# Adaptive max pooling: one flat input in two groups, one reduction per load, three stores

## The chip, the cores and the metric

The kernel runs on one core of one Trainium2 chip. The metric is device time in microseconds, the median of several executions. The span, which the profile uses, goes from the first to the last instruction of the program and is about 1.8 us shorter. A run counts as fast when it is within 1.5% of the fastest run of the same kernel.

## The reference

The length of 4096 is cut into 256 windows of 16, and each window gives its maximum. As a flat array the input is 2,097,152 windows of 16 float32 (134.2 MB), the output one float32 for each (8.39 MB).

```python
batch, channels, length = 32, 256, 4096        # x: float32; output_size = 256
for i in range(output_size):
    start = int(i * length / output_size)
    end = int((i + 1) * length / output_size)
    result[:, :, i] = np.max(x[:, :, start:end], axis=-1)
```

## The kernel before

The 8192 rows are read in three groups of 21 rows per partition, and 128 rows remain. In a group, partition p starts 21 x 16 KB = 336 KB after partition p - 1: that distance is called the *partition pitch* here. A load takes three rows per partition (48 KB) into a ring that holds three such loads, and VectorE reduces each row by itself. The stores are issued after all loads.

```python
    RING = 9
    G = 21
    N_GROUPS = 3
    LOAD = 3
    CUT = 15
    ...
    ring = pool.tile([P, RING, O, W], fp32, tag="ring", name="ring")
    ...
    xg = xf[0:main].rearrange("(g p r) (o w) -> g p r o w", p=P, r=G, w=W)
    ...
    for g in range(N_GROUPS):
        for r in range(0, G, LOAD):
            at = n_read % RING
            nc.sync.dma_start(
                out=ring[:, at : at + LOAD], in_=xg[g][:, r : r + LOAD]
            )
            for i in range(LOAD):
                pooled(outs[g][:, (r + i) * O : (r + i + 1) * O], ring[:, at + i])
            n_read += LOAD
    ...   # the remaining 128 rows: one load of 16 KB per partition, one reduction
    ...   # five stores: groups 0 and 1, group 2 in two parts, the remaining rows
```

## Time and profile before

| | before |
|---|---|
| time | 335.93 us (335.87 to 336.12, 3 runs) |
| span | 334.3 us |
| DMA queue of loads and stores | 98.9% of 16 engines' span |
| VectorE busy | 278.8 us, 83% |
| bytes | 134.2 MB read, 8.39 MB written |

The page of the kernel before, parts 1, 2, 3 and 5. In part 2 each digit is the busy share, in tenths, of one of 40 slices of the span (9 is 90% or more), and the GB/s row is what the 16 DMA engines moved in that slice.

```profile
span 334.3 us, 157 instructions
DVE 278.8 (83%) x64; POOL 0.2 (0%) x4
...
DMA  9899999999999999999999999999999999999997
GB/s 371 382 465 453 400 465 394 453 459 394 465 394 453 459 394 465 394 453 459 394 465 394 453 459 394 465 394 448 459 400 459 400 447 459 400 459 388 437 426 297
...
q1 hardware_dynamic: 3744, 142.48, 98.9%
...
L53 DVE TENSOR_REDUCE out<-ring 128x256 f32<-128x4096 f32 x63 | 274.5, 4412 | 47.6 <-DMA ring<-in_x_dram 47.6
```

DMA is at 9 in 38 of the 40 slices, VectorE (DVE) was busy for 83% of the span, and all of VectorE's 47.6 us of idle time before reductions was ended by the landing of a load. GB/s alternates because a packet is 48 KB and is counted in the slice where it starts; the mean matters. The chain of waits says the same in order of time (start, duration, what):

```profile
1.64 45.82 DMA ring<-in_x_dram
...
47.48 13.08 DVE out L53 x3
...
60.58 30.47 DMA ring<-in_x_dram
...
91.08 13.08 DVE out L53 x3
```

A chain that alternates between DMA and VectorE looks as if both were limits. It isn't so: the links are 43.6 us apart and pass over three loads (30.47 + 13.08 us). The slot that a reduction frees is filled 30.5 us later because two other loads are queued ahead. One load per 14.53 us, 6.29 MB each, is 433 GB/s: that is the period, and three reductions need only 13.08 us of it.

### The profile page before, as it was taken

The numbers are of one execution on the slowest core, as the hardware profiler recorded it, in microseconds if no ns is written. First come the engines' busy times: TensorE is split into PE (matmuls) and PEld (weight loads), VectorE is DVE, ScalarE is ACT, GpSimd is POOL, SyncE is SP. The second block draws the span as 40 slices with busy tenths as digits, with TensorE's granted clock in tenths as the row PEclk, the third lists the DMA queues.
The fourth block names the chain that finished last, engine by engine and source line by source line (L and its number), as shares of the span: only waits on it lengthen the run. The fifth ranks groups of instructions, "written<-read, shape, count | busy, mean of one in ns | idle before, by whom it ended". The sixth has DMA issues, their size and how long they took to land.

```text
span 334.3 us, 157 instructions
## 1 busy us (share of the span) xinstructions
DVE 278.8 (83%) x64; POOL 0.2 (0%) x4
## 2 busy tenths in 40 slices
DVE  0078989898898989889898898989889898988990
POOL 0000000000000000000000000000000000000000
DMA  9899999999999999999999999999999999999997
GB/s 371 382 465 453 400 465 394 453 459 394 465 394 453 459 394 465 394 453 459 394 465 394 453 459 394 465 394 448 459 400 459 400 447 459 400 459 388 437 426 297
DMA packets 3889, 142.62 MB, mean 427 GB/s; under 512 B 432, under 2 KB 560, under 8 KB 688
## 3 DMA queue, kind: packets, MB, share of 16 engines
q1 hardware_dynamic: 3744, 142.48, 98.9%
q10 hardware_dynamic: 144, 0.13, 0.1%
q14 instruction: 1, 0.01, 0.0%
HBM read 134.22 MB, written 8.39 MB: 427 GB/s over the span
## 4 chain that ended last, share of the span: by engine, by line
DMA 68%; DVE 26%; DVEq 2%; SPq 0%; issue 0%
DMA ring<-in_x_dram 68%; DVE out L53 25%; DVEq L109 2%; DVE ring L53 1%; SPq L59 0%
## 5 line engine op out<-in xcount | busy, mean ns | idle before, releaser
L53 DVE TENSOR_REDUCE out<-ring 128x256 f32<-128x4096 f32 x63 | 274.5, 4412 | 47.6 <-DMA ring<-in_x_dram 47.6
L53 DVE TENSOR_REDUCE ring<-ring 128x256 f32<-128x4096 f32 x1 | 4.4, 4410 | 0.0
L95 POOL MEMSET const-bfloat16-1.0<- 128x1 bf16 x1 | 0.1, 101 | 0.0
L95 POOL MEMSET const-uint8-127<- 128x1 uint8 x1 | 0.1, 101 | 0.0
L95 POOL MEMSET const-float32-0.0<- 128x1 f32 x1 | 0.1, 98 | 0.2 <-issue 0.2
L95 POOL MEMSET const-float32-1.0<- 128x1 f32 x1 | 0.1, 98 | 0.0
## 6 DMA issues: line engine op xcount, KB each, us to landing
ring<-in_x_dram SPq DMA_DIRECT2D x21, 6144.0 KB, 30.5
out_dram<-out SPq DMA_DIRECT2D x2, 2688.0 KB, 38.4
ring<-in_x_dram SPq DMA_DIRECT2D x1, 2048.0 KB, 29.5
out_dram<-out SPq DMA_DIRECT2D x1, 1920.0 KB, 38.2
out_dram<-out SPq DMA_DIRECT2D x1, 768.0 KB, 11.2
out_dram<-ring ACTq DMA_DIRECT2D x1, 128.0 KB, 6.4
```

What stands on the lines that cost most here:

```text
L53: nc.vector.reduce_max(out=dst, in_=src, axis=mybir.AxisListType.X)
L95: nc = _bacc.Bacc("TRN2", target_bir_lowering=False, num_devices=1)
L109: with _tile.TileContext(nc) as tc:
```

## The change

The intent: treat input and output as one flat run of windows, cut into two groups of unequal size, so that there are no remaining rows; a load of 760 windows (47.5 KB) per partition is pooled by one instruction; three stores. A partition's share in the two groups is 7600 and 8784 windows of 64 bytes, so the partition pitches are 475 and 549 KB, odd numbers of KB.

```diff
-    RING = 9
-    G = 21
-    N_GROUPS = 3
-    LOAD = 3
-    CUT = 15
+    SLOTS = 3
+    CHUNK = 760
+    GROUPS = [10 * CHUNK, total - 10 * CHUNK]      # total = 16384 windows per partition
+    CUT = 10 * CHUNK
 ... (views, tiles)
-            for i in range(LOAD):
-                pooled(outs[g][:, (r + i) * O : (r + i + 1) * O], ring[:, at + i])
+    for g, n in enumerate(GROUPS):
+        xg = xw[first : first + P * n].rearrange("(p n) w -> p (n w)", p=P)
+        og = ow[first : first + P * n].rearrange("(p n) -> p n", p=P)
+        first += P * n
+        for a in range(0, n, CHUNK):
+            b = min(a + CHUNK, n)
+            slot = ring[:, n_loads % SLOTS, 0 : (b - a) * W]
+            n_loads += 1
+            nc.sync.dma_start(out=slot, in_=xg[:, a * W : b * W])
+            nc.vector.reduce_max(
+                out=outs[g][:, a:b],
+                in_=slot.rearrange("p (n w) -> p n w", w=W),
+                axis=mybir.AxisListType.X,
+            )
+        if g < len(GROUPS) - 1:
+            stores.append((og, outs[g]))
+        else:
+            for a, b in ((0, CUT), (CUT, n)):
+                stores.append((og[:, a:b], outs[g][:, a:b]))
 ... (the five stores go, the three are issued after all loads)
```

More of the change, by code (lines that the diff above doesn't have):

```diff
@@ L27 @@
     W = L // O
-    xf = x.flatten_outer_dims()
-    of = out.flatten_outer_dims()
-    rows = xf.shape[0]
-    assert rows == 64 * P
-    RING = 9
-    G = 21
-    N_GROUPS = 3
-    LOAD = 3
-    CUT = 15
+    total = B * C * O // P
+    SLOTS = 3
+    CHUNK = 760
+    GROUPS = [10 * CHUNK, total - 10 * CHUNK]
+    CUT = 10 * CHUNK
+    assert sum(GROUPS) == total and B * C * O % P == 0
     pool = ctx.enter_context(tc.tile_pool(name="pool", bufs=1))
-    ring = pool.tile([P, RING, O, W], fp32, tag="ring", name="ring")
+    ring = pool.tile([P, SLOTS, CHUNK * W], fp32, tag="ring", name="ring")
@@ L41 @@
     outs = [
-        pool.tile([P, G * O], fp32, tag=f"out{i}", name=f"out{i}")
-        for i in range(N_GROUPS)
-    ]
-    main = N_GROUPS * G * P
-    xg = xf[0:main].rearrange("(g p r) (o w) -> g p r o w", p=P, r=G, w=W)
-    og = of[0:main].rearrange("(g p r) m -> g p (r m)", p=P, r=G)
-    xl = xf[main:rows].rearrange("p (o w) -> p o w", w=W)
-    ol = of[main:rows]
-    def pooled(dst, src):
-        nc.vector.reduce_max(out=dst, in_=src, axis=mybir.AxisListType.X)
-    n_read = 0
-    for g in range(N_GROUPS):
-        for r in range(0, G, LOAD):
-            at = n_read % RING
-            nc.sync.dma_start(
-                out=ring[:, at : at + LOAD], in_=xg[g][:, r : r + LOAD]
-            )
-            for i in range(LOAD):
-                pooled(outs[g][:, (r + i) * O : (r + i + 1) * O], ring[:, at + i])
-            n_read += LOAD
@@ L66 @@
-    at = n_read % RING
-    spare = ring[:, (at + LOAD) % RING].rearrange("p o w -> p (o w)")[:, 0:O]
-    nc.sync.dma_start(out=ring[:, at], in_=xl)
-    pooled(spare, ring[:, at])
-    for g in range(N_GROUPS - 1):
-        nc.sync.dma_start(out=og[g], in_=outs[g])
-    for a, b in ((0, CUT), (CUT, G)):
-        nc.sync.dma_start(
-            out=og[N_GROUPS - 1][:, a * O : b * O],
-            in_=outs[N_GROUPS - 1][:, a * O : b * O],
-        )
-    nc.scalar.dma_start(out=ol, in_=spare)
+        pool.tile([P, n], fp32, tag=f"out{i}", name=f"out{i}")
@@ new lines @@
+        for i, n in enumerate(GROUPS)
+    ]
+    xw = x.flatten_outer_dims().rearrange("r (o w) -> (r o) w", w=W)
+    ow = out.flatten_outer_dims().rearrange("r o -> (r o)")
+    stores = []
+    n_loads = 0
+    first = 0
+    for g, n in enumerate(GROUPS):
[11 more added lines that the diff above has]
+                axis=mybir.AxisListType.X,
+            )
+        if g < len(GROUPS) - 1:
[3 more added lines that the diff above has]
+                stores.append((og[:, a:b], outs[g][:, a:b]))
@@ L82 @@
+    for dst, src in stores:
+        nc.sync.dma_start(out=dst, in_=src)
 _INS = ['x', 'output_size']
```

## The prediction

> **What bounds it now.** The DMA engines. The slice row shows DMA 9 (90% or more) in 38 of 40 slices, and the queue table gives the loads' and stores' queue 98.9% of 16 engines' span. 142.6 MB move at 427 GB/s over a 334.3 us span; windows of the steady stretch show 423 to 446 GB/s, about 434. The chain of waits agrees: a load of 6.29 MB lands every 14.53 us (433 GB/s), while its three reductions take 13.1 us (4.41 us each in the groups), so VectorE waits for every load, 47.6 us in all. The Trainium skill ("DMA: Bandwidth & Descriptors", Where 436 GB/s comes from) puts the SBUF-port ceiling at 435.2 GB/s; the trace agrees, for a 48 KB packet takes 1.818 us on one of 16 engines, 432.6 GB/s together. The same bytes at 435.2 GB/s would be 327.7 us, and about 6 us are start (first packet at 1.7 us, first packets about 0.7 us longer) and end. Nothing that keeps the bytes can win 2%.
>
> **What the change does.**
> - Bytes are the same: 134.2 MB in, 8.39 MB out. Loads stay 22, now 21 of 47.5 KB per partition and one of 26.5 KB. Stores go from five to three (3.89, 3.89, 0.61 MB).
> - Packet times fit about 13 ns + 0.03672 ns per byte (48 KB 1818 ns, 16 KB 615 ns). Eight partitions per engine: loads 8 x (21 x 1.799 + 1.01) = 310.3 us (before: 310.3); stores 8 x (2 x 1.126 + 0.184) = 19.5 us (before 19.6). Sixteen fewer packets per engine save 0.1 to 0.2 us. That is the whole effect on the critical path.
> - VectorE: 4096 elements take 4.409 us, about 0.14 us fixed, so 12160 take 12.81 us instead of 13.1. 64 instructions become 22, saving some 6 us of busy time, off the critical path: it only lengthens waits for loads.
> - The ring stays three loads deep, and the next load is issued 12.8 us after a landing, so the queue still holds a whole load plus 1.6 us. No starving.
> - Tail: last load lands about 314 us as now; the reduction before it runs to about 318.6, the last (424 outputs, 7.2 us) to 325.9. The two large stores keep the DMA busy until about 331, so the last 0.61 MB store, issued at 326, is in time. Ends near 334.
>
> **The risk is the pitch.** Engines read partitions in step, at distances of 475 and 549 KB instead of 336 KB. The skill's page (Latency and other measured facts, row pitch) has copies slowed at 2 MiB and above, almost none at 512 KiB, and repaired by 4 KiB of padding. Both new pitches are odd numbers of KB, so I expect no aliasing; no trace here shows it yet. Store rows of 29.7 KB and 34.3 KB pitch start at multiples of 64 B only; I expect a few ns per packet.
>
> **Prediction:** 335.8 us, range 335.0 to 337.2; faster by over 2%: 1%; within 2%: 92%; slower: 7%.
>
> **What would show each step.** Packet view: 47.5 KB packets at about 1.80 us, 29.7 KB stores about 1.13 us; DMA share of the queue still about 99%, 427 GB/s. Groups: reductions of 12.8 us, busy about 273 us. Chain: loads every 14.4 us, then the last reductions or stores. VectorE's wait for loads rises to about 53 us.
>
> **What would make it wrong.** Load packets well over 1.80 us, uneven among engines or worse in one group than in the other: HBM pitch conflicts. Slow unaligned store packets. A gap in the DMA between the large stores and the last, if the last reductions end after 331 us. A gap between loads, if one long reduction frees a slot later than thought.

## The result, and the profile after

| | before | after |
|---|---|---|
| time, median | 335.94 us (335.76 to 336.12, 6 runs) | 335.83 us (335.73 to 335.90, 6 runs) |
| span | 334.3 us | 334.0 us |
| DMA queue | 98.9% | 99.1% |
| VectorE busy | 278.8 us | 276.3 us |
| idle before reductions | 47.6 us | 49.2 us |

The ratio of after to before is 0.9997, 95% interval 0.9984 to 1.001: the same. A ratio is the mean time of one kernel's fast runs over that of the other's in the same rounds, so not quite the ratio of the medians.

The same parts of the page of the kernel after:

```profile
span 334.0 us, 111 instructions
DVE 276.3 (83%) x22; POOL 0.2 (0%) x4
...
DMA  9999899999999999999998999999999999989997
GB/s 361 390 460 454 384 466 437 402 466 437 402 460 425 419 454 408 443 454 396 454 454 384 466 437 402 466 419 419 460 414 431 454 408 443 454 384 440 443 419 306
...
q1 hardware_dynamic: 3600, 142.61, 99.1%
...
L59 DVE TENSOR_REDUCE out<-ring 128x760 f32<-128x12160 f32 (+1 forms) x22 | 276.3, 12565 | 49.2 <-DMA ring<-in_x_dram 49.2
```

The mean of 12565 ns mixes the 21 long reductions with the short last one; the long ones took 12.82 us. The chain after:

```profile
1.64 45.10 DMA ring<-in_x_dram
...
46.76 12.83 DVE out L59
...
59.61 30.28 DMA ring<-in_x_dram
...
89.91 12.83 DVE out L59
```

Nothing has changed but the size of a load: 14.38 us for 6.23 MB, 433 GB/s again. DMA is still full, VectorE is idle 1.6 us more in all, and the span is 0.3 us shorter. The packets of the trace agree with the forecast: 48,640 bytes took 1799 ns (median; forecast 1.80 us), the 30,400-byte store packets 1.13 us (forecast 1.126 to 1.13).

### The profile page after: what moved, and what is told of

The parts are those of the page before. It is cut to its first block, busy times and chain, and to the rows that moved or that the text cites. A ratio compares the mean times of both kernels' runs of the same rounds, so it can differ in the third digit from the quotient of the medians.

```text
span 334.0 us, 111 instructions
## 1 busy us (share of the span) xinstructions
DVE 276.3 (83%) x22; POOL 0.2 (0%) x4
## 3 DMA queue, kind: packets, MB, share of 16 engines
q1 hardware_dynamic: 3600, 142.61, 99.1%
## 4 chain that ended last, share of the span: by engine, by line
DMA 68%; DVE 27%; DVEq 2%; SPq 0%; issue 0%
DMA ring<-in_x_dram 68%; DVE out L59 27%; DVEq L102 2%; SPq L58 0%
## 5 line engine op out<-in xcount | busy, mean ns | idle before, releaser
L59 DVE TENSOR_REDUCE out<-ring 128x760 f32<-128x12160 f32 (+1 forms) x22 | 276.3, 12565 | 49.2 <-DMA ring<-in_x_dram 49.2
## 6 DMA issues: line engine op xcount, KB each, us to landing
ring<-in_x_dram SPq DMA_DIRECT2D x21, 6080.0 KB, 30.3
```

The source lines that it names most:

```text
L59: nc.vector.reduce_max(out=outs[g][:, a:b], in_=slot.rearrange("p (n w) -> p n w", w=W), axis=mybir.AxisListType.X,)
```

## The experiments

Twelve kernels ran; all results are correct except one. They ask three things: is a DMA engine's time per byte the limit, and nothing else (E3, E4, E7, E8); is the pitch harmless because it is odd, or because no pitch matters (E1, E2, E5, E6, E9 to E11); is the ring's depth what keeps the queue full (E12). Each edit is against the changed kernel unless said otherwise.

### E3: one part of the change alone, the merged reduction

Against the kernel before:

```diff
-            for i in range(LOAD):
-                pooled(outs[g][:, (r + i) * O : (r + i + 1) * O], ring[:, at + i])
+            pooled(
+                outs[g][:, r * O : (r + LOAD) * O],
+                ring[:, at : at + LOAD].rearrange("p l o w -> p (l o) w"),
+            )
```

> The kernel before with one part of the change: one reduction of 768 outputs per load in place of three of 256, pitch 336 KB and five stores kept. My theory (VectorE is off the path): the reduction takes 12.94 us against 13.2 us for three, VectorE busy falls by about 6 us to 273 to 277 us, its wait for loads grows by the same, and the time stays at 335.9 within 0.3 us. Rival (the cheaper pooling paid for a loss by the new pitch): this alone is faster, by up to 6 us, 330 to 334 us.

Measured: 335.78 us, ratio to before 0.9994 (0.9982 to 1.0007). VectorE busy 276.3 us, idle before reductions 49.7 us; a reduction of 768 windows took 12.95 us against 13.08 us for three of 256. The rival, that cheaper pooling paid for a loss elsewhere, falls: the merging alone is worth nothing measurable, so the rest of the change had no loss to hide. The saving on VectorE was 2.5 us and not 6 (see the point by point below).

### E7 and E8: more work for VectorE

A second reduction of the first 64 (E7) or 160 (E8) windows of each load, which writes the same values again:

```diff
+            m = min(64, b - a)          # E8: 160
+            nc.vector.reduce_max(
+                out=outs[g][:, a : a + m],
+                in_=slot[:, 0 : m * W].rearrange("p (n w) -> p n w", w=W),
+                axis=mybir.AxisListType.X,
+            )
```

> The changed kernel with a second reduction of 64 of the 760 outputs per load, same values: VectorE has 1.57 us of idle time per load and gets about 1.2 us more work. My theory (VectorE is off the path): 335.8 us within 0.5 us, VectorE busy about 302 us, its wait for loads about 25 us. Rival (the chain of waits, which alternates loads and reductions, means that both are on the path): 22 x 1.2 us more, about 362 us, or half of that.

> The same with 160 outputs more per load, about 2.8 us: 15.6 us of work per load against a load every 14.39 us. My theory: VectorE becomes the limit, loads wait for slots, period 15.6 us; the last reductions end near 18 + 21 x 15.65 + 10 = 357 us and the time is 359 to 364 us, DMA share down to 92 to 93%. If the transfers also lost time at restarts, more than 364.

Measured: E7 335.86 us, ratio to before 0.9996 (0.9981 to 1.001), VectorE 303.0 us busy (91% of the span), its idle time 24.2 us. E8 360.53 us. The chain of waits, in shares of the span, of E7 and then of E8:

```profile
DMA 66%; DVE 32%; DVEq 0%; SPq 0%; issue 0%
```

```profile
DVE 93%; DMA 5%; DVEq 1%; issue 0%
```

E7 shows how such a chain is read. VectorE is put down for 32% of it and got 27 us more work, and the time did not move. Only when a load's work (15.56 us: 12.74 and 2.82 in the chain) exceeded the 14.38 us that a load takes did the chain become VectorE alone, and the time went up. The DMA queue's share was then 94.6%, where 92 to 93% was expected. The trace shows why: after 140 us, when the loads had come to wait for slots, 402 load packets took longer than they should by over 50 ns (how this is counted is told under E1), 8.85 us per engine, which is 2.5% of the span. The time stayed in its range all the same, because VectorE was the limit.

### E4: one store less

The first store (3.89 MB, group 0) is left out; the result is wrong in that group.

```diff
-    for dst, src in stores:
+    for dst, src in stores[1:]:
```

> The changed kernel without its first store (3.89 MB): the result is wrong on purpose in the first group. My theory (every byte costs on the path, wherever its transfer is issued): eight packets of 1.13 us per engine go, 9.0 us, but the last 0.61 MB store is then no longer hidden behind the rest: the last reduction ends at about 325.6 us, the store is issued then and lands about 3.6 us later, so the span is about 329.5 to 331.5 and the time 331 to 333 us, with a gap in the DMA before the last store. Rival (the stores hide behind the last reductions and cost nothing): 335.8 us.

Measured: 331.11 us, ratio 0.9856 (0.9842 to 0.9869). Windows of the last 40 us, of the kernel after and then of E4 (columns: stretch and its length, VectorE busy and its instructions, POOL busy, clock, DMA share, GB/s):

```profile
310.00:320.00 10.00, 10.00 (x2) 0.00 (x0) 1.00 1.01 433
320.00:326.00 6.00, 5.58 (x1) 0.00 (x0) 1.00 1.01 436
326.00:334.00 8.00, 0.00 (x0) 0.00 (x0) 1.00 0.70 296
```

```profile
310.00:320.00 10.00, 10.00 (x2) 0.00 (x0) 1.00 1.01 433
320.00:326.00 6.00, 5.60 (x1) 0.00 (x0) 1.00 0.19 81
326.00:329.30 3.30, 0.00 (x0) 0.00 (x0) 1.00 0.44 184
```

Stores cost their transfer time: the eight packets of 1.13 us per engine that went are 9.0 us. Of these only 4.7 us were won, because the DMA engines then stood idle for 4.25 us (from 322.2 to 326.5 us in the trace), until the last reduction had ended at 325.6 us and the last store could be issued. In the changed kernel the large stores end at 331.2 us, after the last reduction at 325.6 us, so they cover it. The time lies in the expected range; the span, 329.3 us, is 0.2 us below the one expected.

### E1 and E2: the pitch at a power of two

E1 makes one group of all 16,384 windows: pitch 1024 KB, the same 22 loads and the same store sizes. E2 makes two equal groups: pitch 512 KB.

```diff
-    GROUPS = [10 * CHUNK, total - 10 * CHUNK]
+    GROUPS = [total]                       # E2: [total // 2, total // 2]
-            for a, b in ((0, CUT), (CUT, n)):
+            for a, b in ((0, CUT), (CUT, 2 * CUT), (2 * CUT, n)):   # E1 alone
 ... (E2 keeps this line as it was and sets CUT = 9 * CHUNK)
```

> The changed kernel with one group in place of two: partition pitch 1024 KB, the same 22 loads and the same three store sizes (store pitch 64 KB). Theory A (the pitch is a real danger that the odd pitches of the change avoid): load packets of 47.5 KB go from 1.80 us to between 1.9 and 2.4 us, because the Trainium skill's row-pitch figures fall from 512 KiB to 2 MiB, and the time goes to 350 to 440 us. Theory B (a DMA engine's own rate per byte binds, and HBM has room at any pitch when one core streams): packets stay at 1.80 us and the time at 335.8, within 0.5 us.

> The changed kernel with two equal groups: pitch 512 KB, loads of 10 x 47.5 KB + 37 KB in each group. Theory A: a small slowdown, as the skill's page has 207 against 214 GB/s at 512 KiB: packets 1.80 to 1.87 us, time 336 to 347 us. Theory B: 335.8 within 0.5 us.

Measured: E1 340.69 us, ratio 1.0144 (1.0131 to 1.0158). E2 336.15 us, ratio 1.0008 (0.9993 to 1.0023). Both theories fail on E1: its loss is under 2% but clear of the noise, so the pitch matters and B falls, but the time is far below A's 350 to 440 us. The GB/s row of E1 shows why:

```profile
GB/s 275 401 401 401 418 441 430 430 436 430 436 436 430 436 395 436 424 453 424 436 424 441 436 436 430 430 436 430 447 424 430 430 436 424 436 441 406 420 423 258
```

Only the first four slices (some 35 us) are low throughout; a rate of about 433 GB/s follows at the same pitch. A count of slow packets in the trace says it more sharply. A packet's excess is its duration less 13 ns + 0.0367 ns per byte; slow is an excess over 50 ns. Counted are the load packets after the first 16, which are long in every kernel (590 to 960 ns more on average):

```
                        later slow packets   their excess per engine
before (336 KB)                  1                0.04 us
after (475 and 549 KB)           0                0.00 us
E2 (512 KB)                     44                0.28 us
E11 (1020 KB)                   22                0.20 us
E1 (1024 KB)                   212                4.16 us     138 of them before 40 us
```

The store packets of E1 took 1.127 us as in the kernel after (1.13), so the loads account for it: with the first packets, 4.3 us of excess per engine more than in the kernel after, of a span that is 5.5 us longer. E2's time does not differ measurably. Of E1's 212 packets 138 lie before 40 us, with 2.8 of the 4.16 us; of the others 37 lie from 119 to 126 us and 29 from 279 to 318 us. What caused these later ones was not traced.

### E5 and E6: a restart in the middle, first attempt

E5 (at 1024 KB) and E6 (the odd pitches) put the load of index 11 into the slot of the load before it, which should empty the queue.

```diff
-            slot = ring[:, n_loads % SLOTS, 0 : (b - a) * W]
+            at = (n_loads - (n_loads >= 11)) % SLOTS
+            slot = ring[:, at, 0 : (b - a) * W]
```

> The 1024 KB kernel, with the twelfth load put into the slot of the eleventh, so that the queue runs dry once near 166 us and all 16 engines start again together. [...] Theory A1 (engines in step at this pitch collide, and the delays themselves pull them apart, after which the rate is full): after the restart the same happens again, 50 to 150 packets over 50 ns too long, 3 to 4.5 us more per engine, and the drain costs 3 us or more above what it costs the odd-pitch kernel. Rival A2 (the slow packets belong to the first addresses or to the first microseconds of the execution): after the restart only the first packet of each engine is long, about 0.7 us, and the drain costs the same in both kernels, some 15 to 17 us.

> The changed kernel with the same drain, the control. Both theories: the queue is empty for one reduction and an issue, some 14.5 to 16 us, and the first packets after it are about 0.7 us longer; time 350 to 353 us, no other slow packets.

Measured: E5 348.44 us (347.68 to 350.39), E6 338.56 us. The control missed its forecast of 350 to 353 us: the program's scheduler had issued the following load, whose slot was free, ahead of the held one, so there was no long gap. First packets were long again twice, 16 of them near 175 us and 17 near 205 us, with about 0.67 us of excess per engine each time; another 26 slow packets (0.6 us) lie in the last load, and what caused these was not traced. The edit cost 2.7 us in all (338.56 less 335.83). At 1024 KB the same edit cost 7.75 us, and 157 slow packets came between 160 and 240 us. This points to A1, that slow packets come after every restart at this pitch, but the restart wasn't the clean one that was meant.

### E9 and E10: a clean restart

After the seventh load's reduction VectorE writes one column of all three slots, so that the next three loads have to wait for it. E9 is at 1024 KB (with E1's edit), E10 at the odd pitches.

```diff
+            if n_loads == 7:
+                nc.vector.memset(ring[:, :, 0:1], 0.0)
```

> A clean restart at 1024 KB: after the seventh load's reduction VectorE writes one column of all three slots, so that no later load can be issued before it and all 16 engines stand idle for about 15 us, then start with three loads queued as at the beginning. (In the run before, the scheduler had put a load ahead of the held one, so that the queue ran dry only for about 1 us, twice.) Theory A1 (slow packets come after every restart at this pitch): 50 to 150 packets over 50 ns too long after the restart, 2.5 to 4.5 us per engine with the first packets, time 359 to 363 us. Rival A2 (first addresses or first microseconds): only the 16 first packets, time 355.5 to 357.5 us.

> The control: the changed kernel with the same restart. Both theories: the gap of about 15 us and first packets about 0.7 us longer, 350.5 to 353 us, no other slow packets. The difference to the 1024 KB run without drain and with drain is compared: A1 says the drain costs the 1024 KB kernel 2 to 4 us more.

Measured: E9 363.17 us (362.32 to 364.03), E10 351.69 us. The trace has no packet in flight for 14.2 us in E9 (from 108.8 to 123.1 us) and 14.4 us in E10 (from 104.0 to 118.4 us). The GB/s rows of E9 and then E10, with 9 us per slice:

```profile
GB/s 290 398 371 414 425 435 419 435 435 435 435 322 0 140 382 344 365 425 419 430 446 430 435 430 430 430 425 435 430 435 430 430 430 435 430 435 419 416 440 245
```

```profile
GB/s 350 445 423 417 411 445 445 445 439 445 423 295 0 178 445 445 445 439 428 417 434 417 445 445 445 439 428 411 428 428 445 445 439 434 428 417 422 433 427 313
```

After the zero, E10 is back at 445 GB/s in the second slice; E9 stays at 344 to 382 for three slices. Between 120 and 160 us E9 had 157 slow packets (4.86 us of excess per engine, as against 3.9 us in its first 40 us), E10 after its restart 20, of which 15 are first packets. The memory addresses are other ones than at the start and the execution is long under way, so A2 falls: at 1024 KB a spell of slow packets of some 35 us followed this restart, as it had followed the start. The restart cost 22.5 us there and 15.9 us at the odd pitches. The difference of 6.6 us is larger than the 2 to 4 us expected, and the time 0.2 us above A1's range; slow packets explain about 4.2 us of it. The rest is idle time of the DMA engines: per engine E9 has 17.7 us more of it than E1, and E10 15.3 us more than the changed kernel, 2.4 us apart. Part of that is seen after the gap, where the first 16 packets began within 2.4 us of each other in E9 and within 0.9 us in E10.

### E11: 4 KB less than the power of two

```diff
-    GROUPS = [10 * CHUNK, total - 10 * CHUNK]
+    GROUPS = [total - 64, 64]              # pitches 1020 KB and 4 KB; 23 loads, four stores
```

> One large group of pitch 1020 KB, 4 KB less than the power of two, and the remaining 64 outputs per partition as a second group of pitch 4 KB (23 loads). If what hurts is the power of two, and the skill's remark that 4 KiB of padding restores the rate holds here: no slow packets but the first 16, time 335.8 to 336.5 us. If the size of the pitch (about 1 MB[...]) hurts: about 340.7 us, as at 1024 KB.

Measured: 336.22 us, ratio 1.0005 (0.999 to 1.002). It isn't the size of the pitch: 1020 KB runs as fast as 475. Nor does a pitch have to be odd: 1020 is even, as were the 336 KB of the kernel before. It is not quite clean, with 22 later slow packets where none were expected, 0.2 us in all.

### E12: two slots

```diff
-    SLOTS = 3
+    SLOTS = 2
```

> The changed kernel with two slots in place of three. My theory (the depth of the ring is what keeps the queue full): when a load lands, only one load of 14.39 us is queued; the slot comes free 12.83 us after the landing and the first packets move about 1 us after the issue, [...]so the engines run dry for about 0.5 us and pay about 0.7 us at each restart, 20 times: 355 to 366 us. Rival (a reduction is shorter than a load, so two slots are enough): 336 us.

Measured: 353.93 to 363.17 us in five runs, median 358.36; ratio 1.0547 (1.0526 to 1.0568) from the two timed runs within 1.5% of the fastest (two others were above, and the profiled run, 358.36 us, is not in the ratio). The other kernels did not scatter like this, and the clock was 1.0 throughout; the ratio says little more than "about 5% or more". The timeline of the profiled run (start, duration, engine and line, and in brackets the idle time before):

```profile
62.81 12.82 DVE L59 TENSOR_REDUCE out<-ring 128x760 f32<-128x12160 f32 x1 [1.56 <-DMA ring<-in_x_dram]
78.56 12.82 DVE L59 TENSOR_REDUCE out<-ring 128x760 f32<-128x12160 f32 x1 [2.92 <-DMA ring<-in_x_dram]
92.90 12.82 DVE L59 TENSOR_REDUCE out<-ring 128x760 f32<-128x12160 f32 x1 [1.52 <-DMA ring<-in_x_dram]
108.50 12.82 DVE L59 TENSOR_REDUCE out<-ring 128x760 f32<-128x12160 f32 x1 [2.78 <-DMA ring<-in_x_dram]
```

In this stretch every second load lands about 1.3 us late. The trace has 375 later slow packets, at odd pitches, with 11.9 us of excess per engine, about half of what the span lost (22.6 us): restarts cost long packets even where the pitch is good. The other half is idle time of the DMA engines, 14.4 us per engine where the changed kernel has 3.3 us. The third slot is what keeps the queue filled, though a reduction is shorter than a load.

No version with a correct result beats both kernels: E4 and the packets say that only fewer bytes or fewer idle microseconds of the DMA engines can help, and of these some 3 us are left, 1.7 us before the first packet and 1.3 us after the last (332.7 us of 334.0).

## Why the prediction was right, point by point

- **What bounds the kernel: right, and shown.** The prediction rested on the Trainium skill, "DMA: Bandwidth & Descriptors", section Where 436 GB/s comes from, which puts the ceiling of the SBUF ports at 435.2 GB/s. The packets' slope of 0.03672 ns per byte on each of 16 engines is 435.7 GB/s, and all full windows lie near it. The same section says that for transfers between HBM (the chip's main memory) and SBUF (the core's own) the HBM side, about 358 GB/s for a core, binds; the 433 GB/s measured on this one core lie above that, so the measurement decides. That the limit is in the SBUF ports and not elsewhere on the DMA path is the page's account; no run here separates the two. E4 shows that a removed transfer is worth its time until something else is exposed, and E7 that VectorE's time is worth nothing while a load's work stays below the 14.38 us of a load.
- **The sum of packets: right.** Forecast 310.3 + 19.5 us per engine plus start and end; the last packet ended at 332.7 us. The saving of 0.1 to 0.2 us from sixteen fewer packets per engine fits the span (334.3 to 334.0 us), but the interval of the ratio does not resolve it.
- **VectorE: a term mis-sized, off the critical path.** The prediction had "64 instructions become 22, saving some 6 us of busy time", busy "about 273 us", its wait rising "to about 53 us". Measured: 2.5 us saved, 276.3 us busy, 49.2 us of waits. It charged each of the 42 removed instructions the whole fixed 0.14 us (which the 4.41, 7.21 and 12.82 us of 4096, 6784 and 12,160 elements bear out), but three reductions back to back took 13.08 us and not 3 x 4.41 = 13.23 us: neighbours overlap by some 0.08 us each. E3, which changes nothing else, has the same 276.3 us.
- **The ring: right.** In the changed kernel each load after the first three was issued on the end of a reduction, 30.3 us before it landed, with the queue never dry. E12 shows what the third slot is worth: about 5%.
- **The tail: right, with the margin that it named.** The last reduction ended at 325.6 us (forecast 325.9) and the large stores at 331.2 us (forecast 331). E4 shows the wait that comes when that cover goes.
- **The pitch: right in the verdict; the reason, odd numbers of KB, was not what counts.** The prediction drew on the same page, section Latency and other measured facts, which has copies at 207 GB/s for a row pitch of 512 KiB and 164 for 2 MiB against 214 in full, and 4 KiB of padding as the cure. Here, too, a power of two hurts, 1024 KB, and 4 KB less cures it. But 336 and 1020 KB, both even, run as fast as the odd pitches, and 512 KB was not measurably slower: the kernel would have been safe at these too. The danger was also overrated in E1's expectation: 1024 KB cost only 1.4% in a kernel that streams without a break, because most of the slow packets came in one spell after the start, where the forecast of 350 to 440 us took the loss to be steady.
- **What stays open.** Why the spells end. In E1 the engines' starts had spread from about 1.2 us to some 2 us or more when the first spell ended, so delays pulling the engines out of step is a tempting story. Against it, after the partial restart of E5 the starts were over 4 us apart while packets were still slow (packets sorted to engines by their times, which is rough). E1's later slow packets came with no restart. The address mapping behind this was only argued.

## What to carry to other kernels

Before changing the instructions of an engine that waits for DMA, compare the period of the loads with the engine's work per load: while the work was shorter and the queue never ran dry, neither less work on that engine (E3) nor more (E7) changed the time, however often the chain of waits named it. Try one load more in flight than the arithmetic of load against compute asks for: in E12 short droughts cost idle time and longer packets, some 5% in all. Avoid a partition pitch of 1024 KB, which cost 1.4% here (512 and 1020 KB nothing measurable); a steady stream lost most of it in the first 35 us, but E9, which stopped once, paid again.

## What the Trainium skill lacked or had wrong

- "DMA: Bandwidth & Descriptors", Latency and other measured facts: the row-pitch entry gives one rate for each pitch, of copies from HBM to HBM, and none for 1024 KiB. For loads into SBUF from one core, 1024 KB cost 1.4% in all, most of it in a spell of about 35 us after the start (2.8 of 4.16 us per engine in E1's later packets), and again after the restart of E9; 512 KB was not measurably slower (1.0008). A pitch 4 KB smaller cured it here (1.0005); the page's cure, 4 KiB more, was not run.
- Same section: the first byte on this path is given as about 600 ns. Here the first packet began 0.6 us after the end of the issuing instruction (1.11 to 1.73 us), which agrees, and 1.0 us after its start at 0.73 us. A further cost was found on no page: the first 16 packets took 0.6 to 1.0 us longer than later ones on average, and at the odd pitches about 0.65 us per engine was paid again at a restart (E6, E10).
- "Trainium Kernel Development and Optimization", Best Practices, says to double-buffer. Two slots were about 5% slower than three here, although the reduction (12.82 us) is shorter than the load (14.38 us).
- "HBM Reference", Specifications (TRN2), has about 425 GB/s for a core that streams alone. The 427 GB/s over the whole span, start and end included, agree with it; windows of 24 us and more between start and end of the changed kernel had 431 to 436 GB/s.
